# A decoder layer on one core: other places for the weight parts of gate and up, and one group of tiles with halved products

## The chip, the core and the metric

The kernel runs on one core of a Trainium2 chip. The metric is the device time in microseconds (us) of one execution. Engines are named as the profile names them: PE is TensorE's matrix products, PEld its weight loads, DVE VectorE, ACT ScalarE, POOL GpSimd, SP SyncE.

## The reference

One hybrid decoder layer on 256 tokens of width 2048, in fp32:

```
h  = RMSNorm(x)
z  = h @ W_in            # pool channels | q-latent | kv-latent | rope key | memory query
y  = concat(PoolMixer(z_pool), MLA(z_q, z_kv, z_kr), MemXAttn(z_mq, mem)) @ W_o
x  = x + y
x  = x + ConvGLU(RMSNorm(x))

def conv_glu_ffn(h, w_gate, w_up, conv_w, conv_b, w_down):
    g  = h @ w_gate                                   # 2048 -> 5632
    gc = conv_b + sum_j conv_w[j] * (g shifted by 2 - j)    # j = 0, 1, 2
    return (silu(gc) * (h @ w_up)) @ w_down           # 5632 -> 2048
```

The change is about the two products `h @ w_gate` and `h @ w_up`.

## The kernel before

**Precision.** The products run in the type fp32r, which keeps fewer bits than fp32. So each operand is split into a high part (the value cast to fp32r) and a low part (the value minus the high part), and a product is the sum of three: high by high, high by low and low by high. Weights are split when they are used, by `split_w`: ACT casts `raw` to `wh`, DVE subtracts `wh` from `raw` and writes `wl`.

**The z projection, gate and up** all go through `gemm_t`, with the weights as the stationary operand and the activations as the moving one. An activation buffer holds, for each 128 features, the high parts of the 256 tokens and behind them the low parts. One call makes one output tile of 128 features from 16 chunks of 128 input features:

- The 16 chunks of weights (128 x 2048, 1 MB, one DMA from `load_w`) are split in two halves of eight chunks (`HS` = 1024 columns).
- For each chunk a **high product** loads a chunk of `wh` and moves 512 columns (high and low activations) into the 512 columns of a PSUM bank; a **low product** loads the same chunk of `wl` and moves 256 columns (high activations) into the bank's second half. Later ACT and DVE add the two halves of the bank (`halves`, `half_add`).
- In the first ("even") half the eight high products come first, then the eight low ones. In the second ("odd") half it is the other way round. A tile is therefore 8 high, 8 low, 8 low, 8 high products.

**Places.** A place is the offset, in fp32 elements, at which a part's data begin in their buffer. Before, `wh` begins at 0, `wl` at 48 in the even half and at 16 in the odd half (`shift`), for which its buffer has 64 spare columns. In the built program the stage buffers and the activation buffers all begin at the same remainder of 256 bytes (64 elements), so that a place is also the distance to the moving operand's start, modulo 64; this holds before and after the change.

**Order.** The loop over `f` = 0 to 43 makes for each `f` a gate tile and an up tile (88 tiles in all), and then `glu(f)` on ACT and DVE: scale, convolution over three tokens, SiLU, product, and a new split for the down projection. Three buffers each of `wr`, `wh` and `wl` let the DMA and the split run ahead of PE. `f` = 0 is made in two calls per tile, each on eight chunks, beside the transposes that finish `h2`. The ten tiles of the z projection (`w_z`) use `gemm_t` in the same way; all other products use `gemm_n`, where the activations are the stationary operand, and call `split_w` with no shift.

**Other names.** `ssacc` is the sum of squares of the memory's columns, whose column sums `col_sums` takes early; `rxb` is the row scale of `x` spread over partitions, `krr` the rotated rope key. `L257` is a warm-up of PE at the start: 12 products of a tile of ones with itself. `L216` are the column sums: products that move one column.

Of the kernel before, what the change touches and what calls it, by code (L numbers as in the profile page):

```python
# [23 lines left out]
H = 8  # L24
NOPE = 128
ROPE = 64
# [11 lines left out]
HS = 1024  # L38
NN = 512

PAIRS = KF // 2
SEVEN = tuple(range(2, 20, 2))

VEC = [
    ("g_mix", KD), ("g_ffn", KD), ("g_q_lat", QR // P), ("g_kv_lat", KVR // P),
# [15 lines left out]
def layer(ctx, tc, xT_d, xn_d, memT_d, vec_d, tab_d, w_z_d, w_mqkr_d, w_q_d, w_kv_d, w_mem_d, w_pool_d, w_o_d,  # L61
          w_g_d, w_u_d, w_dn_d, out_d):
    nc = tc.nc

    const = ctx.enter_context(tc.tile_pool(name="const", bufs=1))
    stage = ctx.enter_context(tc.tile_pool(name="stage", bufs=1))
# [5 lines left out]
    def nm(s):  # L72
        uid[0] += 1
        return f"{s}_{uid[0]}"

    def ps_main():
        return psm.tile([P, 512], F32, tag="m", name=nm("psm"))

    def ps_aux():
        return psa.tile([P, 512], F32, tag="a", name=nm("psa"))  # L80

    def load_w(src, n, cut=STG):
        raw = stage.tile([P, STG], F32, tag="wr", name=nm("wr"), bufs=3)
        for c in range(0, n, cut):
            nc.sync.dma_start(raw[:, c:min(n, c + cut)], src[:, c:min(n, c + cut)])
        return raw[:]

    def keep(ins, on=True):

        return tc.keep_in_program_order(ins) if on else ins  # L90

    def split_w(raw, o, n, cut=HS, kept=False, shift=0):

        hi = stage.tile([P, HS], F32R, tag="wh", name=nm("wh"), bufs=3)
        lo = stage.tile([P, HS + 64], F32R, tag="wl", name=nm("wl"), bufs=3)[:, shift:shift + HS]
        for c in range(0, n, cut):
            e = min(n, c + cut)
            keep(nc.scalar.copy(hi[:, c:e], raw[:, o + c:o + e]), kept)  # L98
            keep(nc.vector.tensor_tensor(lo[:, c:e], raw[:, o + c:o + e], hi[:, c:e].bitcast(F32), op=ALU.subtract),  # L99
                 kept)  # L100
        return hi, lo

    def gemm_t(ps, raw, o, act, ks, first=True, last=True, kept=False, between=None):


        ks = list(ks)
        nk = HS // P
        cs = range(0, len(ks), nk)
        for c in cs:
            kc = ks[c:c + nk]  # L110

            hi, lo = split_w(raw, o + c * P, len(kc) * P, shift=16 if c // nk % 2 else 48)

            for low in ((False, True) if c // nk % 2 == 0 else (True, False)):
                for i, k in enumerate(kc):
                    w = (lo if low else hi)[:, i * P:(i + 1) * P]
                    keep(nc.tensor.matmul(ps[:, T if low else 0:2 * T], w, act(k)[:, 0:T] if low else act(k),  # L117
                                          start=first and c + i == 0 and not low,
                                          stop=last and c == cs[-1] and i == len(kc) - 1 and low == (c // nk % 2 == 0),
                                          skip_group_check=True), kept)  # L120
            if between is not None and c == 0:
                between()

# [49 lines left out]
    mp = mix.enter_context(tc.tile_pool(name="mix", bufs=1))  # L173
# [12 lines left out]
    def tok():  # L186
        return mp.tile([P, 512], F32, tag="tok", name=nm("tok"), bufs=3)
# [67 lines left out]
    ps = ps_aux()  # L255
# [24 lines left out]
    pss = [[ps_main()[:] for _ in range(2)] for _ in range(NT)]  # L280
    for c in range(KD // 2):
        raw = raw0 if c == 0 else load_w(w_mem_d[c], STG, HS if c == 1 else STG)
# [16 lines left out]
    ps = ps_aux()  # L299
# [61 lines left out]
    pss = [[ps_aux()[:, :NH] for _ in range(2)] for _ in range(NT)]  # L361
    for c in range(KD // 2):
        raw = load_w(w_mqkr_d[c], 2 * 576)
        for i in range(2):
            hi, lo = split_w(raw, i * 576, 576)
# [9 lines left out]
            x_square(i)  # L375
        if c < 4:
            x_load()
    rxb = mp.tile([P, T], F32, name="rxb")

    def mq_done():  # L380

        x_rstd()
        for tt in range(NT):
            t = tok()
            nc.scalar.copy(t[:, 0:NH], pss[tt][0][:, :NH])
            nc.scalar.copy(t[:, NH:512], pss[tt][1][:, :512 - NH])
            nc.scalar.copy(kr[:, tt, :], pss[tt][1][:, 512 - NH:NH])
            head_sq(fmq3[:, tt], t[:].rearrange("p (h d) -> p h d", d=XD))
            nc.vector.tensor_scalar(fmq3[:, tt], fmq3[:, tt], rx2[:, tt:tt + 1], None, op0=ALU.mult)
            to_features(mqT, t, tt, XH, gqk[:, 1:2])  # L390
        rsqrt_(fmq, fmq, 1.0 / XD)
        for tt in range(NT):
            nc.vector.tensor_scalar(fmq3[:, tt], fmq3[:, tt], rx[:, tt:tt + 1], 1.0 / math.sqrt(XD),
                                    op0=ALU.mult, op1=ALU.mult)


        dx = tok()
        for tt in range(NT):
            nc.vector.tensor_scalar(dx[:, tt * P:(tt + 1) * P], identf[:], rx[:, tt:tt + 1], None, op0=ALU.mult)
        ps = ps_aux()  # L400
        nc.tensor.matmul(ps[:, 0:T], ones[:], dx[:, 0:T], start=True, stop=True)
        nc.scalar.copy(rxb[:], ps[:, 0:T])


    class Head:
# [75 lines left out]
    for m in range(6):  # L481
        raw = load_w(w_z_d[m], STG)
        if m in (1, 3):
            keep(nc.sync.dma_start(x1n[:, m // 2, :], xn_d[m // 2]))
        ps = ps_main()
# [29 lines left out]
    zp = mp.tile([P, 4, T], F32, name="zp")  # L515
    def pool_in(g):
        raw = load_w(w_z_d[6 + g], STG)
        ps = ps_main()
        gemm_t(ps, raw, 0, lambda k: xg[:, k, :], range(KD), kept=g == 0, between=lambda: mem_steps(6 + g))
        half_add(zp[:, g, :], ps)  # L520
        nc.vector.tensor_tensor(zp[:, g, :], zp[:, g, :], rxb[:], op=ALU.mult)


    def pool_mix():
# [60 lines left out]


    sskr, fk, fkn, fkr = sm(NT), sm(NT * H), sm(NT * H), sm(NT * H)
    krr = mp.tile([P, NT, 1, ROPE], F32, name="krr")
    for tt in range(NT):
        head_sq(sskr[:, tt:tt + 1], kr[:, tt:tt + 1, :])  # L590
        rotate(krr[:, tt], kr[:, tt:tt + 1, :], 1, tt, 1)
# [119 lines left out]
    for n in range(4):  # L711
        pss = [[ps_main()[:]] for _ in range(NT)]
# [7 lines left out]
    h2 = big.tile([P, KD, 2 * T], F32R, tag="act", name="h2")  # L720
# [17 lines left out]
    for n in range(4):  # L738
        pss = [[ps_main()[:]] for _ in range(NT)]
# [34 lines left out]
    def glu(f, psg, psu):  # L774
# [8 lines left out]
        j, e = f // 2, f % 2  # L783
        if j not in SEVEN:
            if e == 0:
# [21 lines left out]
    pss = [ps_main() for _ in range(2)]  # L807
# [9 lines left out]
    for f in range(1, KF):  # L817
        pss = []
        for w in (w_g_d, w_u_d):
            raw = load_w(w[f], STG)  # L820
            pss.append(ps_main())
            gemm_t(pss[-1], raw, 0, lambda k: h2[:, k, :], range(KD))
        glu(f, *pss)


# [85 lines left out]
    for c in range(2):  # L911
# [3 lines left out]
        for j in range(PAIRS):  # L915
            kept = c > 0 or j > SEVEN[0]
            if j in SEVEN:
                if com is None:
                    com = [com_ps()[:] for _ in range(4)]
                seven(c, j, own, com, j == SEVEN[0], j == SEVEN[-1], kept)  # L920
            else:
                between = None
                if j == 0 and done is not None:
                    between = lambda o=done: finish(0, o, nc.gpsimd)
                elif j >= PAIRS - 2:
                    between = lambda s=j - PAIRS + 3: common(c, com, s)
# [89 lines left out]
```

## Time and profile before

| | us |
|---|---|
| median of the two runs (1008.01 and 1008.3) | 1008.15 |
| profiled execution, device time | 1008.52 |
| its span, first to last instruction | 1006.7 |
| PE busy | 1001.2 (99%) |
| PEld busy | 863.2 (86%) |
| DVE busy | 751.4 (75%) |
| ACT busy | 577.8 (57%) |

The span runs from the first to the last instruction of the profiled execution. Matrix products overlap in the records, because a product begins before the record of the one ahead ends; what counts is the interval between two starts. A row of the view in order of time merges alike instructions that follow each other: its start, the time from the first start to the last end, and the count. From such a row the interval is (length minus the record of the last product) divided by (count minus one). The gate and up stage runs from 289 to 775 us of the span.

### The profile page before, as it was taken

How to read it: one execution, taken by the hardware profiler on the slowest of the kernel's cores; microseconds unless marked ns; L12 is line 12 of the kernel's file. 1: busy time of each engine (PE TensorE's matmuls, PEld its weight loads, DVE VectorE, ACT ScalarE, POOL GpSimd, SP SyncE). 2: the span in 40 equal slices, each digit the busy share in tenths (PEclk: the TensorE clock that was granted, in tenths of full speed). 3: DMA queues.
4: the chain of work that ended last, by engine and by line, in shares of the span. 5: the costliest groups of instructions: out<-in, count | busy, mean ns of one | idle time of the engine just before them, and what ended most of it. 6: DMA issues, size and time to landing. Idle time of an engine off the chain costs nothing.

```text
span 1006.7 us, 14129 instructions
## 1 busy us (share of the span) xinstructions
PE 1001.2 (99%) x5354; PEld 863.2 (86%) x5354; DVE 751.4 (75%) x1134; ACT 577.8 (57%) x853; POOL 18.5 (2%) x39
## 2 busy tenths in 40 slices
PE   9999999999999999999999999999999999999998
PEld 8898888888888888888888888888888888888886
DVE  6878689855677676776767677676767788888886
ACT  6778666544576555555555555555555565545553
POOL 1010000000000000000000000000000000010000
PEclk9999999999999999999999999999999999999999
DMA  9777344334665555554555555555555765576551
GB/s 361 260 243 297 129 165 178 128 146 145 210 208 210 179 197 193 184 208 172 205 184 195 194 184 209 174 203 185 191 200 201 263 214 191 205 275 212 206 209 42
DMA packets 31764, 200.17 MB, mean 199 GB/s; under 512 B 3664, under 2 KB 4176, under 8 KB 9808
## 3 DMA queue, kind: packets, MB, share of 16 engines
q1 hardware_dynamic: 28512, 189.04, 52.9%
q0 software_dynamic: 2752, 9.44, 2.6%
q8 instruction: 42, 0.69, 0.3%
q10 hardware_dynamic: 432, 0.79, 0.3%
q14 instruction: 26, 0.21, 0.1%
HBM read 195.06 MB, written 4.19 MB: 198 GB/s over the span
## 4 chain that ended last, share of the span: by engine, by line
PE 99%; DVE 0%; ACT 0%; issue 0%
PE psm L117 53%; PE psm L137 5%; PE psm L138 5%; PE psm L139 5%; PE psa L846 4%; PE psm L844 4%; PE psm L845 4%; PE psa L844 4%; PE psa L845 4%; PE psm L846 4%; PE psa L665 1%; PE psa L137 1%; PE psa L139 1%; PE psa L138 1%; PE psa L229 1%; PE psa L257 1%
## 5 line engine op out<-in xcount | busy, mean ns | idle before, releaser
L99 DVE TENSOR_TENSOR wl<-wr,wh 128x1024 fp32r<-128x1024 f32 (+2 forms) x338 | 392.3, 1165 | 63.7 <-ACT wh L98 58.7
L98 ACT CAST wh<-wr 128x1024 fp32r<-128x1024 f32 (+2 forms) x338 | 339.4, 1006 | 136.2 <-PE psm L138 47.3
L117 PE MATMUL psm<-h,wh 128*128 128x512 f32 x1408 | 336.8, 391 | 0.0
L117 PEld LDWEIGHTS psm<-h,wh 128*128 128x128 f32 x1408 | 257.7, 188 | 50.0
L117 PEld LDWEIGHTS psm<-h,wl 128*128 128x128 f32 x1408 | 176.1, 188 | 6.9
L117 PE MATMUL psm<-h,wl 128*128 128x256 f32 x1408 | 177.5, 278 | 0.0
L99 DVE TENSOR_TENSOR wl<-dn,wh 128x1024 fp32r<-128x1024 f32 x58 | 67.8, 1220 | 26.3 <-ACT wh L98 26.3
L98 ACT CAST wh<-dn 128x1024 fp32r<-128x1024 f32 x58 | 59.3, 1052 | 38.3 <-PE psm L845 21.7
L770 ACT COPY g<-psm 128x256 f32<-128x256 f32 x44 | 16.4, 372 | 88.7 <-PE psm L117 88.7
L771 DVE TENSOR_TENSOR g<-g,psm 128x256 f32<-128x256 f32 x44 | 18.5, 420 | 58.7 <-ACT g L770 58.7
L771 DVE TENSOR_TENSOR u<-u,psm 128x256 f32<-128x256 f32 x44 | 18.5, 421 | 52.8 <-ACT u L770 52.8
L781 ACT ACTIVATE gc<-gc 128x256 f32<-128x256 f32 x44 | 18.4, 419 | 63.9 <-DVE gc L780 63.8
L780 DVE SCALAR_TENSOR_TENSOR gc<-g,vec,gc 128x255 f32<-128x255 f32 x88 | 42.1, 478 | 0.3
L844 PE MATMUL psa<-wh,aT 128*128 128x512 f32 x104 | 40.5, 389 | 0.0
L845 PE MATMUL psa<-wh,aT 128*128 128x512 f32 x104 | 40.5, 389 | 0.0
L845 PE MATMUL psm<-wh,aT 128*128 128x512 f32 x104 | 40.5, 389 | 0.0
L846 PE MATMUL psa<-wl,aT 128*128 128x512 f32 x104 | 40.5, 389 | 0.0
L844 PE MATMUL psm<-wh,aT 128*128 128x512 f32 x104 | 40.5, 389 | 0.0
L846 PE MATMUL psm<-wl,aT 128*128 128x512 f32 x104 | 40.5, 389 | 0.0
L117 PE MATMUL psm<-xg,wh 128*128 128x512 f32 x160 | 39.9, 393 | 0.0
L137 PE MATMUL psm<-wh,cat 128*128 128x512 f32 x96 | 38.2, 398 | 0.0
L139 PE MATMUL psm<-wl,cat 128*128 128x512 f32 x96 | 37.4, 390 | 0.0
(227 smaller groups left out, 1393.9 us busy)
## 6 DMA issues: line engine op xcount, KB each, us to landing
wr<-in_w_g SPq DMA_DIRECT2D x44, 1024.0 KB, 4.8
wr<-in_w_u SPq DMA_DIRECT2D x44, 1024.0 KB, 4.8
wr<-in_w_dn SPq DMA_DIRECT2D x33, 1024.0 KB, 4.8
wr<-in_w_o SPq DMA_DIRECT2D x16, 1024.0 KB, 4.9
dn<-in_w_dn SPq DMA_DIRECT2D x11, 1024.0 KB, 4.9
wr<-in_w_z SPq DMA_DIRECT2D x10, 1024.0 KB, 5.5
wr<-in_w_mem SPq DMA_DIRECT2D x6, 1024.0 KB, 7.8
wr<-in_w_mqkr SPq DMA_DIRECT2D x8, 576.0 KB, 4.0
```

The costliest lines, as they stand in the source:

```text
L98: keep(nc.scalar.copy(hi[:, c:e], raw[:, o + c:o + e]), kept)
L99: keep(nc.vector.tensor_tensor(lo[:, c:e], raw[:, o + c:o + e], hi[:, c:e].bitcast(F32), op=ALU.subtract), kept)
L117: keep(nc.tensor.matmul(ps[:, T if low else 0:2 * T], w, act(k)[:, 0:T] if low else act(k), start=first and c + i == 0 and not low, stop=l ...
L137: keep(nc.tensor.matmul(ps, xh, hi[:, i, o], start=first and i == 0, stop=False), kept)
L138: keep(nc.tensor.matmul(ps, xl, hi[:, i, o], start=False, stop=False), kept)
L139: keep(nc.tensor.matmul(ps, xh, lo[:, i, o], start=False, stop=last and i == nk - 1), kept)
L771: nc.vector.tensor_tensor(t[:], t[:], ps[:, T:2 * T], op=ALU.add)
L780: nc.vector.scalar_tensor_tensor(gc[:, d:T], g[:, 0:T - d], v(w, f), gc[:, d:T], op0=ALU.mult, op1=ALU.add)
L781: nc.scalar.activation(gc[:], gc[:], AF.Silu)
L844: nc.tensor.matmul(ps, a[0], b[0], start=first, stop=False)
L845: nc.tensor.matmul(ps, a[1], b[0], start=False, stop=False)
L846: nc.tensor.matmul(ps, a[0], b[1], start=False, stop=last)
```

## The change

- `gemm_t` no longer calls `split_w` but a new `split_t`, which takes a place for the high part and for the low part. The low part may lie in two pieces, each at a place of its own; DVE then writes it with two instructions instead of one.
- A table `PLACES` gives each group of four `f` (eight tiles) its places: group `f // 4`, 0 to 10. The first two numbers are the high part's places in the even and in the odd half. With three numbers, the third says how many of the eight low products in the even half lie at 48; the others lie at 16, modulo 64, and those of the odd half at 16. With four numbers, the last two are the low part's places in the even and in the odd half. Group 9 has the places of before.
- In group 9 (`f` = 36 to 39) each product is made in two: one for each 128 tokens, with the same weights. A high product then moves 2 x 128 columns (high and low activations of these tokens), a low one 128.
- The z projection and `f` = 0 use the default `(0, 0, 4)`.
- The buffers of `wh` and `wl` grow by 64 columns each (three of each). To make room, `rxb` and `krr` share one tile that takes the buffer of `ssacc`.

```diff
+PLACES = ((0, 0, 4), (0, 0, 1), (0, 0, 56, 8), (0, 0, 40, 24), (16, 48, 8), (48, 16, 8), (24, 24, 8), (40, 40, 8), (0, 32, 8),
+          (0, 0, 8), (0, 0, 4))
...
-    def split_w(raw, o, n, cut=HS, kept=False, shift=0):
-        hi = stage.tile([P, HS], F32R, tag="wh", name=nm("wh"), bufs=3)
-        lo = stage.tile([P, HS + 64], F32R, tag="wl", name=nm("wl"), bufs=3)[:, shift:shift + HS]
+    def split_w(raw, o, n, cut=HS, kept=False):
+        hi = stage.tile([P, HS + 64], F32R, tag="wh", name=nm("wh"), bufs=3)[:, 0:HS]
+        lo = stage.tile([P, HS + 128], F32R, tag="wl", name=nm("wl"), bufs=3)[:, 0:HS]
...
+    def split_t(raw, o, n, hi_at, low, kept):
+        hi = stage.tile([P, HS + 64], F32R, tag="wh", name=nm("wh"), bufs=3)[:, hi_at:hi_at + n]
+        lo = stage.tile([P, HS + 128], F32R, tag="wl", name=nm("wl"), bufs=3)
+        e = low[0] * P
+        b = low[1] + e + (low[2] - low[1]) % 64
+        keep(nc.scalar.copy(hi, raw[:, o:o + n]), kept)
+        for d, r in ((low[1], slice(0, e)), (b, slice(e, n))):
+            w = r.stop - r.start
+            if w:
+                keep(nc.vector.tensor_tensor(lo[:, d:d + w], raw[:, o + r.start:o + r.stop], hi[:, r].bitcast(F32),
+                                             op=ALU.subtract), kept)
+        m = n // P
+        return ([hi[:, i * P:(i + 1) * P] for i in range(m)],
+                [lo[:, (low[1] if i < low[0] else b - e) + i * P:][:, :P] for i in range(m)])
...
-            hi, lo = split_w(raw, o + c * P, len(kc) * P, shift=16 if c // nk % 2 else 48)
+            odd = c // nk % 2
+            low = (place[2], 48, 16) if len(place) == 3 else (nk, place[2], 0)
+            if odd:
+                low = (nk, 16, 0) if len(place) == 3 else (nk, place[3], 0)
+            hi, lo = split_t(raw, o + c * P, len(kc) * P, place[odd], low, kept)
...
+                    for t in range(NT):
+                        if low:
+                            r, m = ps[:, T + t * P:T + (t + 1) * P], act(k)[:, t * P:(t + 1) * P]
+                        else:
+                            r, m = (x.rearrange("p (a t) -> p a t", a=2)[:, :, t * P:(t + 1) * P]
+                                    for x in (ps[:], act(k)))
+                        keep(nc.tensor.matmul(r, w, m, start=begin and t == 0, stop=end and t == NT - 1,
+                                              skip_group_check=True), kept)
...
-    rxb = mp.tile([P, T], F32, name="rxb")
+    late = mp.tile([P, 2, T], F32, tag="ssacc", name="late", bufs=1)
+    rxb = late[:, 0, :]
...
-    krr = mp.tile([P, NT, 1, ROPE], F32, name="krr")
+    krr = late[:, 1, 0:NT * ROPE].rearrange("p (t o d) -> p t o d", t=NT, o=1)
...
-            gemm_t(pss[-1], raw, 0, lambda k: h2[:, k, :], range(KD))
+            gemm_t(pss[-1], raw, 0, lambda k: h2[:, k, :], range(KD), place=PLACES[f // 4], narrow=f // 4 == 9)
```

**Where instructions change.** PE at the gate tile and the up tile of `f` = 36, before (`h` is the activation buffer `h2`, `psm` the PSUM bank, `wh` and `wl` the weight parts):

```order
L117 MATMUL psm_6529<-h_2424,wh_6530 128x512 x8
L117 MATMUL psm_6529<-h_2424,wl_6531 128x256 x8
L117 MATMUL psm_6529<-h_2424,wl_6551 128x256 x8
L117 MATMUL psm_6529<-h_2424,wh_6550 128x512 x8
L117 MATMUL psm_6572<-h_2424,wh_6573 128x512 x8
L117 MATMUL psm_6572<-h_2424,wl_6574 128x256 x8
```

The same place after the change:

```order
L157 MATMUL psm_6556<-h_2433,wh_6557 128x2x128 x16
L157 MATMUL psm_6556<-h_2433,wl_6558 128x128 x16
L157 MATMUL psm_6556<-h_2433,wl_6594 128x128 x16
L157 MATMUL psm_6556<-h_2433,wh_6593 128x2x128 x16
L157 MATMUL psm_6631<-h_2433,wh_6632 128x2x128 x16
L157 MATMUL psm_6631<-h_2433,wl_6633 128x128 x16
```

The order of the batches is the same; each batch of eight has become one of sixteen, of half the columns.

DVE at the gate tile of `f` = 4, the first of group 1, before (`g` and `gc` belong to `glu` of `f` = 3):

```order
L771 TENSOR_TENSOR g_3240<-g_3240,psm_3156 128x256
L776 TENSOR_TENSOR g_3240<-g_3240,r_2815 128x256
L99 TENSOR_TENSOR wl_3259<-wr_3255,wh_3258 128x1024
L780 SCALAR_TENSOR_TENSOR gc_3244<-g_3240,vec,gc_3244 128x255
L99 TENSOR_TENSOR wl_3279<-wr_3255,wh_3278 128x1024
```

and after:

```order
L811 TENSOR_TENSOR g_3259<-g_3259,psm_3173 128x256
L816 TENSOR_TENSOR g_3259<-g_3259,r_2824 128x256
L119 TENSOR_TENSOR wl_3278<-wr_3274,wh_3277 128x128
L119 TENSOR_TENSOR wl_3278<-wr_3274,wh_3277 128x896
L820 SCALAR_TENSOR_TENSOR gc_3263<-g_3259,vec,gc_3263 128x255
L119 TENSOR_TENSOR wl_3299<-wr_3274,wh_3298 128x1024
```

The low part of the even half is written in two pieces, 128 columns at place 48 and 896 at 16; the odd half and the work around them stand as before. The DMAs of SP and POOL are the same, in the same order.

More of the change, by code (lines that the diff above doesn't have):

```diff
@@ L101, in split_w, with gemm_t @@
         return hi, lo
-    def gemm_t(ps, raw, o, act, ks, first=True, last=True, kept=False, between=None):
+    def split_t(raw, o, n, hi_at, low, kept):
[12 more added lines that the diff above has]
+                [lo[:, (low[1] if i < low[0] else b - e) + i * P:][:, :P] for i in range(m)])
+    def gemm_t(ps, raw, o, act, ks, first=True, last=True, kept=False, between=None, place=(0, 0, 4), narrow=False):
         ks = list(ks)
@@ L110, in gemm_t @@
             kc = ks[c:c + nk]
-            hi, lo = split_w(raw, o + c * P, len(kc) * P, shift=16 if c // nk % 2 else 48)
-            for low in ((False, True) if c // nk % 2 == 0 else (True, False)):
-                for i, k in enumerate(kc):
[L116 to L120, printed above, removed]
+            odd = c // nk % 2
[3 more added lines that the diff above has]
+            hi, lo = split_t(raw, o + c * P, len(kc) * P, place[odd], low, kept)
+            for low in ((False, True) if odd == 0 else (True, False)):
+                for i, k in enumerate(kc):
+                    w = (lo if low else hi)[i]
+                    begin = first and c + i == 0 and not low
+                    end = last and c == cs[-1] and i == len(kc) - 1 and low == (odd == 0)
+                    if not narrow:
+                        keep(nc.tensor.matmul(ps[:, T if low else 0:2 * T], w, act(k)[:, 0:T] if low else act(k),
+                                              start=begin, stop=end, skip_group_check=True), kept)
+                        continue
+                    for t in range(NT):
[6 more added lines that the diff above has]
+                                              skip_group_check=True), kept)
             if between is not None and c == 0:
@@ L401, in mq_done @@
         nc.tensor.matmul(ps[:, 0:T], ones[:], dx[:, 0:T], start=True, stop=True)
-        nc.scalar.copy(rxb[:], ps[:, 0:T])
+        nc.scalar.copy(rxb, ps[:, 0:T])
     class Head:
@@ L520, in pool_in @@
         half_add(zp[:, g, :], ps)
-        nc.vector.tensor_tensor(zp[:, g, :], zp[:, g, :], rxb[:], op=ALU.mult)
+        nc.vector.tensor_tensor(zp[:, g, :], zp[:, g, :], rxb, op=ALU.mult)
     def pool_mix():
```

## The prediction

> **What bounds the kernel now.** I read the page first: the busy shares, the granted clock and the chain of work that ended last.
>
> ```profile
> span 1006.7 us, 14129 instructions
> PE 1001.2 (99%) x5354; PEld 863.2 (86%) x5354; DVE 751.4 (75%) x1134; ACT 577.8 (57%) x853; POOL 18.5 (2%) x39
> PEclk9999999999999999999999999999999999999999
> PE 99%; DVE 0%; ACT 0%; issue 0%
> ```
>
> The chain is TensorE from end to end, at an undivided clock, so what the change does to the interval from one product's start to the next is what it does to the time. The share of 99% alone says little, because records of products overlap. So I went on to the order in time. Four views of PE show one gate tile and part of the next; columns are start, length from first start to last end, and the count of merged instructions.
>
> ```profile
> start us, us, engine line op out<-in xcount [idle before <-releaser]
> 499.72 1.98 PE L117 MATMUL psm<-h,wh 128*128 128x512 f32 x8
> 501.54 0.98 PE L117 MATMUL psm<-h,wl 128*128 128x256 f32 x7
> 502.36 1.07 PE L117 MATMUL psm<-h,wl 128*128 128x256 f32 x8
> 503.38 1.32 PE L117 MATMUL psm<-h,wh 128*128 128x512 f32 x5
> ```
>
> The next answer is the table by stage, cut where the four batches of that tile begin: length of the stretch, then busy time by engine.
>
> ```profile
> 499.72:501.53 1.81, 1.81 (x9) 1.50 (x8) 0.42 (x1) 0.37 (x1) 1.00 0.62 122
> 501.53:502.47 0.94, 0.94 (x9) 0.93 (x8) 0.00 (x0) 0.00 (x0) 1.00 1.01 427
> 502.47:503.38 0.91, 0.91 (x10) 0.91 (x9) 0.00 (x0) 0.00 (x0) 1.00 1.00 423
> 503.38:505.22 1.84, 1.84 (x10) 1.51 (x9) 0.00 (x0) 0.00 (x0) 1.00 0.30 58
> sum 5.50, PE 5.50 PEld 4.86 DVE 0.42 ACT 0.37; mean PE 1.38 PEld 1.21 DVE 0.11 ACT 0.09
> ```
>
> A tile takes 5.50 us, in batches of eight: high parts of the even half 1.81, its low parts 0.94, low parts of the odd half 0.91, its high parts 1.84. Intervals come from the merged rows, less the record of the last one (0.39 us for 512 columns, 0.28 for 256). They are (1.98 - 0.39)/7 = 0.227 us for 512 columns; (0.98 - 0.28)/6 = 0.117 for 256 columns with the low part at place 48; (1.07 - 0.28)/7 = 0.113 at place 16; and (1.32 - 0.39)/4 = 0.2325 for the first high products after the low ones. The two commonest intervals are in the ratio of their columns (0.227/512 = 0.113/256 = 0.44 ns a column): there the moving operand sets the pace, and the weight load is hidden. At place 48 the same product takes 4 ns more. So **place matters in this trace**, but over what it could give back, 8 x 0.004 in the low parts and about 0.03 in the high parts of the odd half, a tile has 0.06 us to lose.
>
> The other engines have slack in the steady stretch of this stage:
>
> ```profile
> 305.00:774.00 469.00, 469.00 (x2730) 413.91 (x2730) 337.69 (x498) 261.20 (x376) 0.00 (x0) 1.00 0.54 191
> ```
>
> DVE works 337.69 of 469 us (72%), ACT 261.20 (56%), DMA 54%.
>
> **Part 1: the group with halved products.** Tiles f = 36 to 39, gate and up, are eight tiles. Each of their 32 products becomes two, with the same weights: 32 high ones that move 2 x 128 columns, and 32 low ones that move 128. What a second product with equal weights costs depends first on whether its weights are loaded again. They are, as the warm-up shows: its source line L257 issues 12 products with one and the same tile as weights (a plain fp32 product leaves two records).
>
> ```profile
> L257 PE MATMUL psa<-ones 128*128 128x128 f32 x24 | 5.5, 428 | 1.1 <-DVE eps L164 1.1
> L257 PEld LDWEIGHTS psa<-ones 128*128 128x128 f32 x24 | 5.2, 331 | 1.1 <-DVE eps L164 1.1
> ```
>
> As many loads as products, though the weights never changed. Then the question is how fast loads can follow each other when the moving part is too short to cover them. The column sums answer it, since they move one single column (also fp32, so two records each):
>
> ```profile
> 123.48 0.81 PE L216 MATMUL psa<-ones,zs 128*128 128x1 f32 x6
> L216 PEld LDWEIGHTS psa<-ones,zs 128*128 128x128 f32 x8 | 1.1, 192 | 0.1
> L117 PEld LDWEIGHTS psm<-h,wl 128*128 128x128 f32 x1408 | 176.1, 188 | 6.9
> ```
>
> Six records, the last one 0.25 us long, give (0.81 - 0.25)/5 = 0.112 us each. Their load's record is 192 ns, that of the gate's low parts 188: the same kind of load. So I take **0.112 us as the floor of any product with a full load**, and a product of 128 columns, which needs only 128 x 0.44 = 57 ns for moving, sits on it.
>
> - Low parts: 32 x 0.112 = 3.58 us in place of 0.94 + 0.91 = 1.85, so +1.73. Lower end: none of the loads faster than that row, +1.73. Upper end: each also pays what the 256-column ones pay at place 48, 32 x 0.117 = 3.74, +1.89.
> - High parts: each half moves 256 columns, like the low products of before. No row has a high part with 256 columns, so between 32 x 0.113 = 3.62 and 32 x 0.117 = 3.74, in place of 1.81 + 1.84 = 3.65: -0.03 to +0.09. I take the middle, +0.03.
>
> A tile gains 1.76 us (1.70 to 1.98), eight of them **14.1 us** (13.6 to 15.8). Nothing can hide this: PE is the chain. The other engines only get more time, 7.3 us a tile instead of 5.50.
>
> **Part 2: known places.** By default, thus in the z projection, groups 0 and 10 and the first tiles, four of the eight low products in the even half go from place 48 to 16; in group 1 seven. At 4 ns each that is 16 x 4 x 0.004 (groups 0 and 10) + 8 x 7 x 0.004 (group 1) + 10 x 4 x 0.004 (z) = **-0.6 us**. The price is that the low part of those halves is subtracted in two instructions on DVE:
>
> ```profile
> L99 DVE TENSOR_TENSOR wl<-wr,wh 128x1024 fp32r<-128x1024 f32 x300 | 365.4, 1222 | 55.9 <-ACT wh L98 51.0
> L99 DVE TENSOR_TENSOR wl<-wr,wh 128x512 fp32r<-128x512 f32 x22 | 15.0, 685 | 0.6 <-ACT wh L98 0.5
> ```
>
> 2 x 685 - 1222 = 148 ns more in each of 36 halves, 5.3 us on DVE. I cost it at nothing: it lies in DVE's free 28%. In the z projection, where the low part has a shorter lead, its worst is 10 x 0.148 = 1.5 us, if PE stood still for all of it.
>
> **Part 3: places that no row shows.** Groups 2 to 8, 56 tiles, put low parts at 56, 8, 40 and 24, and high parts at 16, 48, 24, 40 and 32. From below: all low products at 0.113 and all high ones at 0.227 make 16 x 0.340 = 5.44, -0.06 a tile, -3.4 us for 56. From above, the slowest rows of this shape. For 512 columns that is the 0.2325 above. For 256 it is a batch of the z projection, which follows on products of another type:
>
> ```profile
> 110.03 1.19 PE L117 MATMUL psm<-xg,wl 128*128 128x256 f32 x8
> ```
>
> (1.19 - 0.28)/7 = 0.130 us. Then a tile takes 16 x (0.2325 + 0.130) = 5.80, +0.30, and 56 tiles +16.8 us. I stay near the rows of steady work, since the high products have 0.227 - 0.112 = 0.115 us of room for a slower load and the low ones none: low ones at 0.115 on average (16 x 0.115 = 1.84, no change), and five more slow high products in each tile (5 x 0.006 = 0.03) make +0.03 a tile, **+1.7 us**.
>
> [...]
>
> **Part 4: the shared tile** of the row scale and the rotated key takes the buffer of the squares' sum.
>
> ```profile
> L216 PE MATMUL psa<-ones,ssacc x4: 164/250/250, 50.3 to 50.5; 128*128 128x1 f32 x4
> ```
>
> Its last reader is done at 50.8 us, and the first write stands behind the products of the memory query, which start only then; nothing waits. The larger stage buffers shift the others by 1536 bytes, six times 256, so no remainder of 256 bytes changes.
>
> **Sum.** 14.1 - 0.6 + 1.7 = +15.2 us. The profiled execution took 1008.52 us (its span 1006.7 and 1.8 around it), 0.4 above the median of the two runs, 1008.15. So 1008.5 + 15.2 = 1023.7 as a profile, and **1023.4 us** as a median, 1.5% slower, less than the 2% (20.2 us) that I take for what a measurement tells from no change.
>
> **The rivals.**
> - *A wrong place stalls the loads (slower by over 2%).* If a load that starts off a multiple of 16 elements takes longer, each low product waits for it. Everything up to the other parts is +13.5; the limit of 1028.3 is passed when groups 2 to 8 add more than 6.7 us, 0.12 us a tile or 3.7 ns a product. With the slow rows (0.30 a tile) at half of the 56 tiles it is 8.4 us, 1030; with all, 1038. For it: two places that were tried differ by 4 ns, and six have never been seen. Against it: 16 of the 32 products cover a load twice over. 0.14.
> - *The second half is cheaper than a full load.* If the load of equal weights were short, a pair of low products would take 0.112 + 0.057 = 0.169 us, 16 of them 2.70, +0.85 a tile, and the high ones -0.03: +6.6 for eight tiles, 1008.2 + 6.6 + 1.1 = 1016. Against it stands L257, for it only that no fp32r row has 128 columns. 0.10. [...]
> - *The places take away the 0.44 ns a column.* Then all could become faster; but the rate is the same at 256 and 512 columns, with loads beside all or half of it, so it does not come from the loads. At most the -0.06 a tile above. 0.01 for faster by over 2%.
>
> **Chances.** My forecast has 0.75, the rivals 0.14, 0.10 and 0.01. Range 1015 to 1033: it takes in part 1's and part 3's bounds near the forecast, the cheap halves and the lower half of the slow places. Faster by over 2% 0.01, within 2% 0.85, slower by over 2% 0.14.
>
> **What would show it.** The eight tiles of f = 36 to 39 should take 7.3 us each, with low products 0.112 us apart and as many loads as products; at 4.5 us for their low parts or under 3 part 1 is wrong. Tiles of groups 0, 1 and 10 should stay within 0.05 us of 5.50, each of groups 2 to 8 between 5.44 and 5.60. PE should have no new wait on DVE. I am wrong if a group of places stands at 5.7 or more, or if the interval of the 512-column products changes with the high part's place.

## The result: 1092.5 us, 8.4% slower

| | before | after |
|---|---|---|
| median, us | 1008.15 | 1092.47 (two runs, 1092.08 and 1092.87) |
| ratio | | 1.0837 [1.0814, 1.086] |
| profiled execution, us | 1008.52 | 1092.87 |
| its span, us | 1006.7 | 1091.1 |

The forecast was 1023.4, the range 1015 to 1033. The page of after, in the lines that answer to those of before: the head, the busy shares, TensorE's share in 40 slices, the granted clock, and the chain.

```profile
span 1091.1 us, 14666 instructions
PE 1044.8 (96%) x5610; PEld 901.7 (83%) x5610; DVE 756.8 (69%) x1170; ACT 578.7 (53%) x853; POOL 18.5 (2%) x39
PE   9995666999999999999999999999999999999998
PEclk9997778999999999999999999999999999999999
PE 94%; ACT 3%; DVE 1%; DMA 1%; issue 0%; ACTq 0%
```

Something is wrong from the fourth to the seventh slice, 82 to 191 us, long before the gate and up projections: TensorE is busy for little more than half, and its clock is down to 0.7. The table by stage says how much it is. First before, then after; columns are the stretch, its length, busy time (and instructions) of PE, PEld, DVE, ACT and POOL, the granted clock, the share of DMA and GB/s. The rows are the z projection (its ten tiles, whose products read `xg`, with the products of the memory heads and some of the next projection among them), the stage behind it, gate and up, and the rest.

```profile
77.40:163.90 86.50, 86.44 (x491) 74.70 (x490) 68.89 (x154) 60.50 (x114) 0.00 (x0) 1.00 0.52 190
163.90:288.80 124.90, 124.87 (x618) 104.70 (x617) 84.20 (x152) 67.37 (x122) 3.52 (x7) 1.00 0.48 165
288.80:774.50 485.70, 485.69 (x2829) 428.35 (x2828) 349.82 (x521) 274.27 (x401) 0.81 (x2) 1.00 0.54 192
774.50:1006.70 232.20, 227.88 (x1004) 186.87 (x1002) 192.40 (x203) 120.38 (x127) 6.46 (x12) 1.00 0.57 204
```

```profile
77.10:227.80 150.70, 109.86 (x491) 90.65 (x490) 72.13 (x165) 61.79 (x114) 0.00 (x0) 0.83 0.30 108
227.80:352.70 124.90, 124.88 (x618) 104.72 (x617) 84.36 (x154) 67.37 (x122) 3.51 (x7) 1.00 0.48 165
352.70:858.90 506.20, 506.19 (x3085) 451.29 (x3084) 352.32 (x545) 274.75 (x401) 0.83 (x2) 1.00 0.53 184
858.90:1091.10 232.20, 227.88 (x1004) 186.83 (x1002) 192.41 (x203) 120.37 (x126) 6.45 (x12) 1.00 0.58 204
```

Gate and up took 20.5 us more (506.2 - 485.7), 5 above the forecast for the whole change. The other **64.2 us are in the z projection** (150.7 - 86.5), with the same 491 products. The view of waits in that stretch gives the first cause. Columns: what waited for what, us in total, times, the longest. Before, PE has no row in this view.

```profile
PE psm L147 <- DVE wl L119: 23.8, 6, 5.1
PE psm L147 <- ACT wh L115: 13.7, 5, 2.8
PE psm L175 <- ACT wh L103: 3.4, 1, 3.4
```

That is 40.9 us of waits. In order of time, one tile of the z projection shows what PE waits for. First before, in the tile with the scores of the first memory heads (`p` are ACT's exponentials of these scores):

```profile
86.65 1.03 ACT L98 CAST wh<-wr 128x1024 fp32r<-128x1024 f32 x1
87.03 1.89 PE L450 MATMUL psa<-mkT,mqT 128*128 128x256 f32 x8
87.72 1.22 DVE L99 TENSOR_TENSOR wl<-wr,wh 128x1024 fp32r<-128x1024 f32 x1 [0.27 <-ACT wh L98]
88.57 1.27 PE L117 MATMUL psm<-xg,wl 128*128 128x256 f32 x8
90.04 0.56 ACT L423 ACTIVATE p<-psa,st,small 128x256 f32<-128x256 f32 x1 [1.05 <-DVE st L421]
```

The cast at 86.65 begins 3.4 us ahead of the first exponential (90.04), and it isn't for the low products at 88.57: its subtraction ends at 88.94, after these have begun. By the order of ACT's instructions, shown with the second experiment, it is for the odd half of the next tile. Casts run up to a whole tile ahead of TensorE. The same place after:

```profile
91.11 1.03 ACT L115 CAST wh<-wr 128x1024 fp32r<-128x1024 f32 x1
92.20 3.44 PE L147 MATMUL psm<-xg,wh 128*128 128x512 f32 x8 [2.70 <-ACT wh L115]
96.41 1.89 PE L490 MATMUL psa<-mkT,mqT 128*128 128x256 f32 x8
98.86 0.56 ACT L463 ACTIVATE p<-psa,st,small 128x256 f32<-128x256 f32 x1 [5.42 <-DVE st L461]
101.04 1.05 ACT L115 CAST wh<-wr 128x1024 fp32r<-128x1024 f32 x1
102.12 1.22 DVE L119 TENSOR_TENSOR wl<-wr,wh 128x1024 fp32r<-128x1024 f32 x1
103.39 2.08 PE L147 MATMUL psm<-xg,wl 128*128 128x256 f32 x8 [5.10 <-DVE wl L119]
105.27 3.62 PE L147 MATMUL psm<-xg,wh 128*128 128x512 f32 x8
```

Now the odd half's cast stands behind the four exponentials of this very tile (98.86 to 101.04), though ACT had waited 5.42 us before them with the weights in place. The subtraction follows at once, and TensorE starts 5.10 us late. The even half's cast at 91.11 is late in the same way, behind the copy of the tile before: 2.70 us. The last row shows the second cause: eight products of 512 columns take 3.62 us instead of the 1.98 of a batch at full clock, without a wait between them.

**What the change did to the order.** The diff replaces a call of `split_w` *without* `kept` by one of `split_t` with `kept` as its last argument. In seven tiles (`m` = 0 to 5 of the memory heads, and the first z tile) `kept` is true, and there `split_t` now lists its casts and subtractions among the instructions that must stay in the order of the program. The program writes the odd half's split behind `between()`, the memory steps.

### The profile page after: what moved, and what is told of

The parts are those of the page before. It is cut to its first block, busy times and chain, and to the rows that moved or that the text cites. A ratio compares the mean times of both kernels' runs of the same rounds, so it can differ in the third digit from the quotient of the medians.

```text
span 1091.1 us, 14666 instructions
## 1 busy us (share of the span) xinstructions
PE 1044.8 (96%) x5610; PEld 901.7 (83%) x5610; DVE 756.8 (69%) x1170; ACT 578.7 (53%) x853; POOL 18.5 (2%) x39
## 4 chain that ended last, share of the span: by engine, by line
PE 94%; ACT 3%; DVE 1%; DMA 1%; issue 0%; ACTq 0%
PE psm L147 48%; PE psm L157 5%; PE psm L175 5%; PE psm L177 5%; PE psm L176 5%; PE psm L886 3%; PE psa L886 3%; PE psa L885 3%; PE psm L884 3%; PE psm L885 3%; PE psa L884 3%; ACT wh L115 1%; PE psa L705 1%; DVE wl L119 1%; DMA wr<-in_w_z 1%; PE psa L481 1%
## 5 line engine op out<-in xcount | busy, mean ns | idle before, releaser
L147 PE MATMUL psm<-h,wh 128*128 128x512 f32 x1280 | 309.3, 393 | 0.0
L119 DVE TENSOR_TENSOR wl<-wr,wh 128x1024 fp32r<-128x1024 f32 (+3 forms) x232 | 242.7, 1057 | 28.1 <-ACT wh L115 19.3
L115 ACT CAST wh<-wr 128x1024 fp32r<-128x1024 f32 x196 | 205.6, 1050 | 23.9 <-PE psm L147 10.1
L103 ACT CAST wh<-wr 128x1024 fp32r<-128x1024 f32 (+2 forms) x142 | 133.4, 942 | 113.5 <-PE psm L176 39.9
L104 DVE TENSOR_TENSOR wl<-wr,wh 128x1024 fp32r<-128x1024 f32 (+2 forms) x142 | 152.7, 1084 | 46.2 <-ACT wh L103 45.8
L147 PE MATMUL psm<-xg,wh 128*128 128x512 f32 x160 | 54.6, 494 | 13.7 <-ACT wh L115 13.7
L147 PEld LDWEIGHTS psm<-xg,wh 128*128 128x128 f32 x160 | 38.2, 250 | 24.3 <-ACT wh L115 16.4
L147 PE MATMUL psm<-xg,wl 128*128 128x256 f32 x160 | 29.0, 340 | 23.8 <-DVE wl L119 23.8
L147 PEld LDWEIGHTS psm<-xg,wl 128*128 128x128 f32 x160 | 27.3, 245 | 26.8 <-DVE wl L119 25.6
L884 PE MATMUL psa<-wh,aT 128*128 128x512 f32 x104 | 40.5, 389 | 0.0
L885 PE MATMUL psm<-wh,aT 128*128 128x512 f32 x104 | 40.5, 389 | 0.0
```

The lines of the kernel that those rows point to most:

```text
L115: keep(nc.scalar.copy(hi, raw[:, o:o + n]), kept)
L119: keep(nc.vector.tensor_tensor(lo[:, d:d + w], raw[:, o + r.start:o + r.stop], hi[:, r].bitcast(F32), op=ALU.subtract), kept)
L884: nc.tensor.matmul(ps, a[0], b[0], start=first, stop=False)
L885: nc.tensor.matmul(ps, a[1], b[0], start=False, stop=False)
```

## The experiments

### The splits free again

The changed kernel, with one argument changed back:

```
-            hi, lo = split_t(raw, o + c * P, len(kc) * P, place[odd], low, kept)
+            hi, lo = split_t(raw, o + c * P, len(kc) * P, place[odd], low, False)
```

> The changed kernel, but the cast and the subtraction of the weights in gemm_t are no longer held in program order. Theory A (the 64 us lost ahead of gate and up come from holding them, since the casts of the next half then stand behind the copy that ends the tile): the z stage takes 87 us again, and 1092.5 - 64 = 1028 us are left, all of the rest in gate and up (+20.5). Rival B (the two-piece subtraction, the shared tile or the larger buffers cost the 64 us): 1085 us or more, and the z stage stays at 150 us.

Measured: 1028.66 us, ratio 1.0203 [1.0188, 1.0218]. Its z projection and its gate and up:

```profile
77.10:163.70 86.60, 86.60 (x492) 74.86 (x490) 70.05 (x165) 60.59 (x114) 0.00 (x0) 1.00 0.53 189
288.70:794.80 506.10, 506.09 (x3083) 451.18 (x3082) 352.26 (x545) 274.77 (x401) 0.77 (x2) 1.00 0.52 184
```

The z projection is back at 86.6 us, PE's waits are gone, the clock is 1.00; gate and up is as in the changed kernel. One argument carries 63.8 of the 84.3 us. The low part in two pieces, which this kernel keeps (DVE 70.05 against 68.89 us), costs nothing in the z projection.

### The order alone, in the kernel before

```
-            hi, lo = split_w(raw, o + c * P, len(kc) * P, shift=16 if c // nk % 2 else 48)
+            hi, lo = split_w(raw, o + c * P, len(kc) * P, shift=16 if c // nk % 2 else 48, kept=kept)
```

> The kernel before, with one argument added: the splits of gemm_t are held in program order wherever its products are (seven of the ten z tiles). Theory A: the z stage goes from 87 to about 150 us and the time to 1008 + 64 = 1072 us, with a TensorE clock of 0.5 in pieces of that stage. Rival B: 1008 to 1011 us, the cause is elsewhere in the change.

Measured: 1074.19 us (1072.19 to 1076.05), ratio 1.0661 [1.0643, 1.0679]. PE's waits, and the z projection in the table by stage:

```profile
PE psm L117 <- DVE wl L99: 23.2, 6, 5.1
PE psm L117 <- ACT wh L98: 13.7, 5, 2.8
PE psm L137 <- ACT wh L98: 3.4, 1, 3.4
```

```profile
77.00:227.60 150.60, 110.32 (x491) 90.79 (x490) 70.84 (x152) 61.24 (x111) 0.00 (x0) 0.83 0.29 108
```

The waits of the changed kernel to within 0.6 us, and its z projection, without any of its places, pieces or halves. ACT's instructions in program order show the move (`-` is the kernel before, `+` this one; `hadd` is the copy of a finished tile, `p` the exponentials):

```
+L98 CAST wh_909<-wr_844 128x1024
 L472 COPY hadd_930<-psm_846 128x256
-L98 CAST wh_1018<-wr_1015 128x1024
 L491 ACTIVATE zs<-z_929 128x256
 L147 ACTIVATE zl<-z_929,vec 128x256
-L98 CAST wh_1045<-wr_1015 128x1024
+L98 CAST wh_940<-wr_936 128x1024
 L423 ACT_TABLE_LOAD
 L423 ACTIVATE p_963,st_964<-psa_960,st_964,small 128x256 x2
 L423 ACTIVATE p_976,st_977<-psa_973,st_977,small 128x256 x2
+L98 CAST wh_986<-wr_936 128x1024
 L472 COPY hadd_1007<-psm_939 128x256
```

`wh_940` and `wh_986` are the two halves of one tile. Left free, the tile's casts were issued before `hadd_930`, and those of the next tile (`wh_1018`, `wh_1045`) stood where these two stand now.

### Casts alone, subtractions alone

In `split_w` of the last kernel only one of the two instructions is held in order:

```
 keep(nc.scalar.copy(hi[:, c:e], raw[:, o + c:o + e]), kept)             # casts: kept, subtractions: False
 keep(nc.vector.tensor_tensor(lo[:, c:e], ..., op=ALU.subtract), False)  # and the other way round
```

> The kernel before, in which only the casts (ACT) of the seven kept tiles are held in program order; the subtractions (DVE) stay free. Theory 1 (the cast is what comes late, held behind the copy and the exponentials of the half before; the subtraction that follows it at once only hands its lateness on): all of the loss is here, 1068 to 1078, the z projection 148 to 152 us, and TensorE waits some 40 us there, 23 of them on DVE. Theory 2 (the subtractions are held behind DVE's own work on the memory heads, as the larger sum of the waits, on DVE, says): 1008 to 1030, with 13.7 us of waits on ACT at most.

> The kernel before, in which only the subtractions (DVE) of the seven kept tiles are held in program order; the casts (ACT) stay free. Theory 1 (the casts make the loss): within 1% of 1008, the z projection under 92 us, since the casts still run one half ahead. Theory 2 (the subtractions make it): 1040 or more, TensorE waiting 20 us or more on DVE in the z projection, and few or no waits on ACT.

Casts alone: 1068.46 us, 1.0598 [1.0582, 1.0614]. Subtractions alone: 1047.91, 1.0389 [1.0372, 1.0407]. The waits of the first (besides the single one of 3.4 us, as above) and its z projection:

```profile
PE psm L117 <- DVE wl L99: 19.6, 6, 5.1
PE psm L117 <- ACT wh L98: 13.7, 5, 2.8
```

```profile
76.60:222.70 146.10, 109.48 (x492) 90.09 (x491) 71.06 (x154) 61.47 (x113) 0.00 (x0) 0.84 0.30 112
```

and of the second:

```profile
PE psm L117 <- DVE wl L99: 26.6, 10, 4.9
```

```profile
77.40:206.70 129.30, 102.67 (x491) 85.08 (x490) 70.61 (x156) 61.27 (x114) 0.00 (x0) 0.87 0.34 126
```

The edited line is in `split_w`, which the down projection calls too; there it changes nothing, since all that stands behind the z projection takes 842.7 and 842.9 us in these two kernels and 842.8 in the kernel before. Theory 1 is right that the casts alone make nearly all of the loss, 60.5 of 66.0 us (z projection 2 us under its range). It is wrong that the subtractions would be harmless: with the casts free, DVE's program order puts each subtraction behind the memory heads' reductions, and TensorE waits for that instead. The two don't add (60.5 + 39.9 against 66.0), since the waits are in part the same. Either engine's order suffices to lose the cover. The rows that say DVE also don't say whose lateness it is: 19.6 of their 23.2 us come with the casts alone.

### Waits and clock

Of the 64 us only 41 are waits. In slices of 0.6 us of the changed kernel's z projection the clock changes at 84.88, 88.30, 91.71, 95.12, 101.95 and 108.78 us (an estimate from the mean clock of the slice in which each change falls, 0.52 to 0.90): 3.41 or 3.42 us apart, or 6.83, twice that. The stage cut into pieces of 3.41 us, which begin 0.07 us behind these changes:

```profile
81.54:84.95 3.41, 0.00 (x0) 0.00 (x0) 2.73 (x14) 2.10 (x4) 0.00 (x0) 0.99 0.01 2
84.95:88.36 3.41, 3.41 (x12) 3.12 (x13) 0.00 (x0) 0.00 (x0) 0.00 (x0) 0.51 0.67 226
88.36:91.78 3.42, 1.14 (x5) 0.60 (x4) 0.91 (x2) 1.76 (x4) 0.00 (x0) 0.99 0.93 388
91.78:95.19 3.41, 2.99 (x7) 2.42 (x8) 1.29 (x2) 1.65 (x2) 0.00 (x0) 0.51 0.03 7
95.19:98.60 3.41, 3.10 (x18) 2.46 (x17) 1.02 (x3) 0.00 (x0) 0.00 (x0) 1.00 0.00 0
98.60:102.02 3.42, 0.00 (x0) 0.00 (x0) 2.29 (x10) 3.16 (x9) 0.00 (x0) 0.99 0.00 0
102.02:105.43 3.41, 2.04 (x9) 2.04 (x10) 1.22 (x1) 0.06 (x1) 0.00 (x0) 0.50 0.31 55
105.43:108.84 3.41, 3.41 (x9) 2.15 (x7) 0.00 (x0) 0.00 (x0) 0.00 (x0) 0.51 0.60 252
```

The clock (third column from the right) is 0.99 to 1.00 or 0.50 to 0.51 in these pieces, and it follows the piece before: after 0.00, 1.14 and 2.04 us of busy TensorE comes a piece at one half, after 2.99, 3.10 or 3.41 one at full. So these waits are paid twice, at the time and in the products behind them (a batch of 3.62 us instead of 1.98).

The busy time is not all that counts. Two later pieces of the same stage:

```profile
125.84:129.26 3.42, 2.62 (x6) 2.14 (x7) 1.61 (x3) 0.74 (x1) 0.00 (x0) 0.50 0.00 0
173.63:177.04 3.41, 2.02 (x13) 1.84 (x14) 2.43 (x3) 1.03 (x2) 0.00 (x0) 1.00 0.25 60
```

The first, itself at half clock and busy for 2.62 us, is followed by half again; the second, at full clock and busy for only 2.02, keeps the full clock. The piece of 2.04 us above was at half clock too. A piece at full clock from 180.46, busy for 2.00 us, is followed by half (0.50 from 183.88). In this stage the full clock was kept after pieces with 1.93 us of busy TensorE (from 170.22), 1.95 (from 132.67) and 2.02, and lost after the one with 2.00; at half clock, 2.62 us did not win it back and 2.99 did. No run here shows where the limits lie.

To tell the two apart, products that belong to no sum were put into the tiles whose order is held (all in the kernel of the second experiment): ten in each half, with the half's high parts as weights.

```
+            if between is not None and kept:
+                fill = ps_main()
+                for i in range(10):
+                    keep(nc.tensor.matmul(fill[:], hi[:, (i % 8) * P:(i % 8 + 1) * P], act(kc[i % 8]), start=True,
+                                          stop=True, skip_group_check=True), kept)
             if between is not None and c == 0:
                 between()
```

> As e2_pin_only, with ten more products of 512 columns (nobody reads them) behind each half of the seven tiles whose splits are held: 2.3 us of work for gaps of 2.7 to 5.5 us, 32 us of PE work in all. Theory A1 (the slow clock follows from PE's idle gaps and is a part of the loss): the clock stays at 1.0 through the z stage, and the kernel takes 10 to 20 us LESS than e2_pin_only, though it does 32 us more. Rival A2 (the loss is the waits alone, the clock costs nothing of weight): the same as e2_pin_only within 3 us, or more by what does not fit the gaps.

Measured: 1084.43 us, ratio 1.0752 [1.0736, 1.0768], clock 0.985. That is 10 us more than without fillers, where A1 forecast 10 to 20 less and a clock of 1.0. It decides nothing between the two theories, because the first ten stood at the wrong place: ahead of `between()` they push back the memory heads' scores, on which ACT's exponentials and thus the late cast depend. The wait that they were to fill moved along.

```profile
PE psm L117 <- DVE wl L99: 26.9, 7, 5.1
PE psm L117 <- ACT wh L98: 2.0, 5, 0.5
```

The ten at the tile's end did cover theirs (ACT 13.7 to 2.0 us). The next kernel has the same lines behind `between()`:

> The kernel before, with the splits of the seven kept tiles held in program order, and in each of these tiles 20 products of 512 columns that belong to no sum: ten right ahead of the odd half's low products (where TensorE waited 5.1 us for the subtraction) and ten at the tile's end (which then stand ahead of the next tile's first product, where it waited 2.7 us for the cast). They add 7 x 20 x 0.227 = 32 us of work. Theory 1 (of 66 us that the order costs, some 40 are waits and some 24 a clock that falls because of the waits): the fillers lie in the waits, the clock stays near 1.0 and the run takes 10 to 24 us less than the 1074.2 of the kernel whose order alone is changed, 1050 to 1064, though it does more. Theory 2 (the clock has nothing to do with it, only the chain of casts and subtractions sets the time): 1074 as without fillers, or more, clock unchanged at 0.976.

Measured: 1058.49 us, ratio 1.0498 [1.0484, 1.0513]; the waits, and the z projection:

```profile
PE psm L117 <- DVE wl L99: 10.9, 7, 2.8
PE psm L117 <- ACT wh L98: 2.4, 5, 0.5
```

```profile
77.20:212.30 135.10, 121.85 (x631) 100.05 (x630) 71.22 (x155) 61.95 (x114) 0.00 (x0) 1.00 0.34 121
```

With 140 products more (140 x 0.227 = 31.8 us) the kernel is 15.7 us *faster* than without them, and the clock is 1.00. The sums: 86.5 of work + 31.8 + 13.3 of waits = 131.6, where 135.1 is measured; without fillers 86.5 + 40.3 = 126.8, where 150.6 is measured. Of the 23.8 us that are missing there, 3.5 are left as soon as TensorE is kept busy; these are not the clock's. The clock record of the changed kernel, whose z projection has the same waits and length (40.9 and 150.7 us), says the same without fillers: between 84.89 and 190.70 us it has 15 pieces of 3.41 us at 0.50, in which TensorE is busy for 44.2 us. At full clock that is work of 22.1 us (an estimate, at half the time), so 22.1 us are lost. By both, the clock takes 20 to 22 us. Theory 1 holds.

### Gate and up: the halved group alone, the places alone

The kernel of the first experiment without the places (all low parts of the even half at 48, of the odd half at 16, high parts at 0, as before), thus the halved group alone:

```
-            gemm_t(..., place=PLACES[f // 4], narrow=f // 4 == 9)
+            gemm_t(..., place=(0, 0, 8), narrow=f // 4 == 9)     # halved group alone
+            gemm_t(..., place=PLACES[f // 4])                    # places alone
```

> Group 9 with halved products alone: all places as before the change, splits not held. By the trace of the changed kernel its eight tiles take 7.41 us in place of 5.50: 1008.2 + 8 x 1.91 = 1023.5 us. The prediction's own term was 14.1: 1022.3. Rival (weights that are equal are loaded cheaply when nothing else is wrong): 1016 or less.

> The changed kernel with free splits and no halved products, thus the places alone. If the two parts of the gate and up projections add up: 1028.7 less the 15.3 of the halved group, 1013.4 us, 5.2 above the kernel before, and groups as in the changed kernel (5.53 to 5.63 us a tile, group 9 at 5.50). If the halved group disturbs its neighbours or the places cost more without it, the sum isn't met by more than 1 us.

Measured: the halved group 1023.24 us, 1.015 [1.0135, 1.0165], thus +15.0; the places 1013.74, 1.0054 [1.004, 1.0067], thus +5.6. Together 20.6, where the first experiment has 20.4: they add. In the changed kernel, a tile of group 0, all eight of group 7 and all eight of the halved group:

```profile
387.71:393.25 5.54, 5.54 (x34) 4.89 (x32) 3.62 (x6) 2.78 (x4) 0.00 (x0) 1.00 0.69 213
666.03:711.04 45.01, 45.01 (x257) 39.15 (x256) 31.91 (x47) 24.52 (x35) 0.00 (x0) 1.00 0.54 187
755.50:814.75 59.25, 59.25 (x514) 59.24 (x512) 32.49 (x48) 24.73 (x35) 0.00 (x0) 1.00 0.43 146
```

Per tile 5.54, 5.63 and 7.41 us, where every group before has 5.50. In the halved group the weight load is as busy as the products (59.24 of 59.25).

The places one by one, in the changed kernel with free splits and no halved products:

```
-PLACES = ((0, 0, 4), (0, 0, 1), ...)
+PLACES = ((0, 0, 48, 16), (0, 0, 16, 16), (0, 0, 16, 48), (0, 0, 48, 48), (0, 0, 0, 16), (0, 0, 48, 0), (0, 0, 32, 32),
+          (0, 0, 0, 0), (0, 0, 32, 16), (0, 32, 48, 16), (0, 48, 48, 16))
```

> The changed kernel with free splits and no halved products; each of the eleven groups of four tiles has one place for each half's low part and one for each half's high part. (high even, high odd, low even, low odd): group 0 (0,0,48,16) as in the kernel before; 1 (0,0,16,16); 2 (0,0,16,48); 3 (0,0,48,48); 4 (0,0,0,16); 5 (0,0,48,0); 6 (0,0,32,32); 7 (0,0,0,0); 8 (0,0,32,16); 9 (0,32,48,16); 10 (0,48,48,16). Theory A (the place of the low part itself sets the interval, 16 is the fast one): group 1 has both low batches at 0.91 and a tile 5.47; group 3 both at 0.94 and 5.53. Theory B (what counts is the step from the even half's low part to the odd half's, 48 to 16): only groups 0, 9 and 10 have an odd low batch of 0.91, all others 0.94 and 5.53. Theory C (a multiple of 64 bytes, thus 0, 16, 32 and 48, is as good as another, and the first low batch is slow because it follows the high ones): all low batches odd 0.91, even 0.94, a tile 5.50 in all groups but 9 and 10.

Measured: 1012.61 us in the one run, 4.5 more than before. From start to start of TensorE's products in the trace, us per tile and per batch, in steady tiles:

| places: high even, odd; low even, odd | tile | high even | low even | low odd | high odd |
|---|---|---|---|---|---|
| 0, 0; 48, 16 (as before) | 5.50 | 1.81 | 0.94 | 0.91 | 1.84 |
| 0, 0; 16, 16 | 5.54 | 1.81 | 0.94 | 0.94 | 1.84 |
| 0, 0; 16, 48 | 5.57 | 1.82 | 0.94 | 0.94 | 1.87 |
| 0, 0; 48, 48 | 5.57 | 1.82 | 0.94 | 0.94 | 1.87 |
| 0, 0; 0, 16 | 5.55 | 1.81 | 0.95 | 0.94 | 1.84 |
| 0, 0; 48, 0 | 5.55 | 1.81 | 0.94 | 0.95 | 1.84 |
| 0, 0; 32, 32 | 5.57 | 1.82 | 0.96 | 0.96 | 1.82 |
| 0, 0; 0, 0 | 5.57 | 1.81 | 0.95 | 0.96 | 1.84 |
| 0, 0; 32, 16 | 5.53 | 1.82 | 0.96 | 0.91 | 1.84 |
| 0, 32; 48, 16 | 5.55 | 1.84 | 0.94 | 0.91 | 1.86 |
| 0, 48; 48, 16 | 5.51 | 1.82 | 0.94 | 0.91 | 1.83 |

Theory A falls: with both halves at 16, both low batches take 0.94. Theory C falls as well. Theory B is near, not exact: 0.91 comes only with the odd half at 16 and the even half's low part higher, at 48 or at 32; from 0 or 16 to 16 it is 0.94. So in this run a batch's pace (0.91 or 0.94 at the same place 16) goes with the pair of places, not with its own alone. Nor does the pair of low places suffice: groups 4 and 7 of the changed kernel keep 48 and 16, with the high parts at 16 and 48 and at 40, and their odd low batch takes 0.94. Why, no run here shows, and it stays open. None of the eleven beats the pair that the kernel before has; the differences are 0.01 to 0.07 us a tile, at most 6 us over 88 tiles.

## Why the prediction was wrong

- **The step that failed is part 2, "I cost it at nothing".** It asked what the split costs in DVE's time, and bounded that in the z projection by 10 x 0.148 = 1.5 us. On that, it was right: two pieces with free splits cost nothing there. It did not ask *when* the split is issued. "PE should have no new wait on DVE" is what failed, 23.8 us on DVE and 17.1 on ACT.
- **The order of instructions was read in gate and up alone.** It was shown at a gate tile, where `kept` is false and nothing had moved; the sentence there that the work around stands as before holds only there. The last argument in the diff and ACT's order in the z projection would have told it. No rival had it, so the range of 1015 to 1033 had no room for it.
- **How it could have been priced.** In the rows of before, PE ends the scores at 88.92 (87.03 + 1.89), and the exponentials run from 90.04 to 92.22, where ACT's next copy starts. A cast that must stand behind them, 1.03, and its subtraction, 1.22, end at 94.47: an estimate of 5.6 us of waiting for this tile. The changed kernel had 5.10: the exponentials end at 101.04, cast and subtraction (1.05 and 1.22) bring that to 103.31, within 0.1 us of the 103.39 at which the odd half starts, and PE had run dry at 98.29. That gives the waits. The 20 to 22 us of the clock could not be taken from a profile whose clock is 1.00 in every stage; they show in the runs in which TensorE stood still for about 40 us of the z projection (clock 0.83).
- **Part 1 was right in mechanism and nearly in size:** 15.0 us by the run with the halved group alone, 14.1 forecast. The view in order of time and the group of the low products (busy time, mean ns of one):

```profile
772.23 3.69 PE L157 MATMUL psm<-h,wl 128*128 128x128 f32 x32
```

```profile
L157 PE MATMUL psm<-h,wl 128*128 128x128 f32 x256 | 29.5, 273 | 0.0
```

  (3.69 - 0.27)/31 = 0.110 us, where 0.112 was forecast from the column sums: the floor taken from fp32 products holds for these fp32r ones too, with 512 loads in the group's row of 59.25 us. Two halves take 0.220 us at this pace, not 0.169, so the rival with the cheap second half is out. The high halves were mis-sized: 1.92 + 1.96 = 3.88 a tile where the bounds were 3.62 to 3.74. That is 0.121 us for 256 columns, above both rows from which the bounds were taken; no run shows why.
- **The known places had the wrong sign.** -0.6 us was forecast; groups 0, 1 and 10 went from 5.50 to 5.54. The 4 ns between places 48 and 16 had been put down to the place of the product itself. The even half gained nothing at 16 (0.94 in both), and the odd half lost its 0.91 when the even half no longer lay at 48.
- **Part 3 was right in sign, too small.** Groups 2 to 8 stand between 5.53 and 5.63, where 5.44 to 5.60 was expected and 5.7 was the point of being wrong; places as a whole took 5.6 us, not 1.1. The interval of the 512-column products does change with the high part's place, which the prediction had named as a sign against it: a batch in the even half takes 1.81 us with it at 0, 0.227 each, and 1.87 at 24 and 40, 0.234 each. The batch ahead counts here too: in the table, with the high part at 0, the odd one takes 1.84 us behind low products at 16 and 1.87 behind those at 48.
- **The rival on the other side** (a wrong place stalls the loads, 1030) did not happen: its limit was 6.7 us in groups 2 to 8. With free splits the kernel still lies at 1028.66, 2.0% above before, near that rival's price for other reasons. It would have lain in the range, and that by the range's width: the halved group and the places were forecast at 15.2 us and took 20.4.

The sum: 66 (order) + 15.0 (halved group) + 5.6 (places) = 86.6, where 84.3 was measured. The 2 us too many are within the spread of the run with the order alone, whose executions took 1072.2 to 1076.1 with a granted clock of 0.976 to 0.972; its profiled one, at 1072.2, has the same z projection as the changed kernel.

## What to carry to other kernels

An edit to the work ahead of the products has two prices: its time on its engine, and its place in that engine's order; read both, in every stage that calls the edited function, and there with the arguments that this stage passes. Preparing weights up to a tile ahead is what kept TensorE's chain whole here: whatever holds it behind work that itself waits for TensorE (exponentials of scores, a copy of a finished sum) turns the slack of a stage (30% on ACT, 20% on DVE in this one) into a wait in each tile. And price a wait of TensorE with what it does to the clock: here some 40 us of waits cost 20 to 22 us more in the products behind them, half a us for each, by the slower clock (0.83 in the z projection); the 13.3 us of waits among the fillers left it at 1.00.

## What was not expected of the hardware

- Fillers that compute nothing made a kernel faster, 1074.2 to 1058.5 us with 31.8 us more of TensorE's work; the clock of its z projection was 1.00 with them and 0.83 without.
- In the changed kernel's z projection the clock of a piece of 3.41 us went with the piece before, with its busy time and its own clock: 1.14 us of work at full clock was too little to keep it, 2.00 was once too little, and yet 1.93 once enough; at half clock 2.62 us was too little to win it back, and 2.99 was enough.
- In the run of the places one by one, a low batch's time went with the place of the batch ahead of it: with the high parts at 0, 0.91 us at place 16 after 48 or 32, 0.94 after 0 or 16.
